# Two token streams on one core: where the second stream stands during attention, and when both streams' scores are emitted

## The chip, the core and the metric

The kernel runs on one core of a Trainium2 chip. The metric is the device time of one execution in microseconds, taken as the median of several executions. The engines are named as in the profile: PE (TensorE matmuls), PEld (TensorE weight loads), DVE (VectorE), ACT (ScalarE), POOL (GpSimd), SP (SyncE, which issues the DMAs).

## What is computed

Four layers of one block (layers 0 to 3) and then two layers of a second block, on 256 tokens of width 1024, in float32. Cut to what matters here:

```python
for i in range(4):                       # first block
    q, k, v, ... = split(x @ w_in[i])    # kind i % 3: indexed top-k, dilated, plain causal
    mix = attention(rope(q), rope(k), v) # 12 heads of 64 columns
    mo  = memory_attention(qm, mk, mv)   # 4 heads over 256 memory tokens
    x = layer_norm(a * x + concat(mix, mo) @ w_out[i])
    x = layer_norm(a * x + swiglu(x, w_gate_up[i], w_down[i]))
for l in range(2):                       # second block: three attentions, gates, output
    u = rms_norm(x) @ w_in_2[l]
    oa, ob, oc = diff_attention, mla_attention, sliding_window_attention
    x = x + rms_norm(gated_sum(oa, ob, oc) @ w_out_2[l]); x = x + gate(x) * (p[l] @ w_ple_proj[l])
```

In layers 0 and 3 each query first scores all keys with 8 small index heads, and keeps the 64 best keys; the attention of the layer sees only those.

## The kernel before

**Two streams.** The 256 tokens are two halves of 128, stream 0 and stream 1, each run by a generator of its own (`stream(t)`, t = 0 or 1). Stream 0 attends to its own 128 keys, stream 1 to all 256, so stream 1's scores are twice as wide. Both use the same weights. These are read from memory in units of 256 rows by 512 columns or less (`Unit`; there are 600). `ensure` issues a unit's DMA on SP into a `raw` buffer (3 of them), has ACT cast it to a high part H (line 333) and DVE subtract that from it to a low part L (line 334); H and L have 7 buffers each. `gemm_part` then makes, for each of a unit's two blocks of 128 rows, three matmuls (H by the high part of x, L by the same, H by the low part, lines 378 to 380): six matmuls for a unit and a stream. The loop at the end of the program takes a unit of stream 0, splits the weights that it needs, and lets stream 1 go on while its unit's place in the sequence is at most that of stream 0 minus `LAG`, which is 4. So each unit is used by stream 0 and, four units later, by stream 1.

**What sets the order of the attention.** After each unit of a stream `tick(t)` moves that stream's clock on by one, and runs what was put off to that time by `defer` and `job`. A head job of two heads a side has the stages a (score matmuls into two PSUM tiles `w`, then the softmax on DVE and ACT, `softmax_of`), b (transposes of the probabilities on PE, line 500, then a copy) and c (matmuls with the values, line 511, then the division by the sums), one unit of its stream apart. `job` starts one job a stream after the other. So in the code a stage of stream 0 stands directly behind a unit of stream 0, and the same stage of stream 1 behind the same unit of stream 1, four units later.

**Scores.** A score matmul (line 476) contracts over 64 rows, half of the array. `scores` emits, for two sides of heads, a matmul on the upper 64 rows and one on the lower 64 in turn. Each of them appears as two rows in the trace, so x4 in the order is x8 in the trace. Each stream has two PSUM tiles `w`, used for scores, for transposes and for the values' result, and two tiles `mm` for the units.

**Index selection.** In layers 0 and 3 `index_jobs` makes the index scores of 8 heads in two groups (ACT's Relu at line 768, sums on DVE at lines 771 and 773), then eight rounds of the eight largest (line 782) and their replacement (line 783) on DVE, two rounds at a unit, and a mask.

**Softmax.** With a mask or bias DVE adds it and finds the minimum (line 487); without one (the memory heads) it finds the minimum alone (line 483). ACT takes the exponential (line 491). Both engines do their work in the order of the program, and the casts and subtractions of weights are between.

Of the kernel before, what the change touches and what calls it, by code (L numbers as in the profile page):

```python
# [31 lines left out]

LAG = 4
QI_WAIT = 2
IDX_WAIT = 1
# [16 lines left out]
class Unit:  # L52
    def __init__(self, chunk, kt0, nkt, seq):
        self.chunk, self.kt0, self.nkt, self.seq = chunk, kt0, nkt, seq

# [10 lines left out]
def tile_two_blocks(  # L66
# [157 lines left out]

    seq = [0]

    def add_units(ck, groups, step=2, at=None):
        made = []
        for g0, gn in groups:
            for k0 in range(g0, g0 + gn, step):  # L230
                made.append(len(units))
                units.append(Unit(ck, k0, min(step, g0 + gn - k0), seq[0] if at is None else at))
                seq[0] += at is None
        return made
# [11 lines left out]
    def out_chunks(w, late):  # L246
        cks = [Chunk(w, [(0, 512)]), Chunk(w, [(512, 1024)])]
        early = [g for g in ((0, 4), (6, 2)) if g[0] != late] if late == 4 else [(0, 2), (6, 2)]
        order = [add_units(ck, early) for ck in cks]
        rest = [(4, 2)] if late == 4 else [(2, 4)]  # L250
        return cks, order, [add_units(ck, rest) for ck in cks]

    plan1, plan2 = [], []
    for i in range(DEPTH):
# [3 lines left out]
        if kind == 0:  # L258
            pl["qi"] = chunk(w, (2304, 2816))
            pl["wk"] = chunk(w, (2816, 3144))  # L260
            pl["v0"] = chunk(w, (1536, 2048))
            pl["v1"] = chunk(w, (2048, 2304))
        else:
            pl["v1"] = chunk(w, (2048, 2560))
            pl["v0"] = chunk(w, (1536, 2048))
        if kind == 1:
# [24 lines left out]
    for l in range(DEPTH_2):  # L291
        pl = {}
        w = w_in_2[l]
        pl["b"] = chunk(w, (2048, 2464))
        pl["aq"] = chunk(w, (0, 512))
# [6 lines left out]
        pl["zb"] = chunk(w, (2464, 2976))  # L302
        pl["za"] = chunk(w, (1536, 2048))
# [42 lines left out]

    def job(t, *stages, span=1):
        at = max(now[t] + 1, started[t] + 1)
        started[t] = at + span - 1
        for k, fn in enumerate(stages):  # L350
            defer(t, fn, at=at + k)
        return at + len(stages)

    def tick(t):
        now[t] += 1
        run_until(t, now[t])

    def run_until(t, at):
        q = queues[t]
        while q and q[0][0] <= at:  # L360
            heapq.heappop(q)[2]()

    def finish(t, at):
        while queues[t] and queues[t][0][0] <= at:
            heapq.heappop(queues[t])[2]()

# [277 lines left out]
    def attend_job(t, nk, *sides):  # L644
# [3 lines left out]
        def a():  # L648
            made = scores(t, *[(d["q"], d["k"]) for d in sides])
            for x, d, s in zip(st, sides, made):  # L650
                x["sums"] = d["sums"] if "sums" in d else small(2, "sums", bufs=4)
                bias = d.get("bias")
                x["sm"] = softmax_of(t, s, n, nk, bias() if callable(bias) else bias, x["sums"],
                                     inits=d.get("inits"), mins=d.get("mins"))

# [6 lines left out]

        return job(t, a, b, *[lambda i=i: c(i) for i in range(len(sides))], span=len(sides))


    def block1(t):
# [6 lines left out]
        for i in range(DEPTH):  # L673
# [42 lines left out]
            def dilated_job(s0):  # L716
# [16 lines left out]
                def a0():  # L733
                    made = scores(t, *sides((0, 1)))
                    for (_, _, d), s in zip(heads, made):
                        d["sm"] = work_tile([P, 3, nk], "sm", 2)
                        d["mn"], d["sum"] = small(3, "mn3"), small(1, "rsum")
                        masked(d, s, 0, 0)
                        masked(d, s, 1, 1)

                def a1():
                    made = scores(t, *sides((2,)))
                    for (_, _, d), s in zip(heads, made):
                        masked(d, s, 0, 2)
                        sm = d["sm"]
                        act.activation(sm, sm, AF.Exp, bias=d["mn"][:, 2:3], scale=-1.0, accum_out=d["sum"])
                        vec.tensor_tensor(out=sm[:, 1], in0=sm[:, 1], in1=sm[:, 2], op=ALU.add)
                        vec.tensor_tensor(out=sm[:, 0], in0=sm[:, 0], in1=sm[:, 1], op=ALU.add)

# [8 lines left out]

                return job(t, a0, a1, b, c, span=2)

            def index_jobs(wi):
                def group(g):
                    halves = [([4 * g + e, 4 * g + 2 + e], half_slice(e)) for e in range(2)]
                    made = scores(t, *[([qiT[r, h // 2, :] for h in hs], [[k[r, :] for k in kiTs]] * 2)
                                       for hs, r in halves])
                    for (hs, _), s in zip(halves, made):
                        rl = work_tile([P, 2, nk], "sm", 2)
                        act.activation(rl, s[:, :, :nk], AF.Relu)
                        for e, h in enumerate(hs):
                            if h == 0:  # L770
                                vec.tensor_scalar(score[:, :nk], rl[:, e], wi[:, 0:1], None, op0=ALU.mult)
                            else:
                                vec.scalar_tensor_tensor(out=score[:, :nk], in0=rl[:, e], scalar=wi[:, h : h + 1],
                                                         in1=score[:, :nk], op0=ALU.mult, op1=ALU.add)

# [74 lines left out]
            if kind == 1:  # L850
                for s in range(2):
                    for c, dst in enumerate((qT, kT)):
                        acc = yield from gemm(t, pl["qk"][2 * s + c], *xT)
# [6 lines left out]
            else:  # L860
                for g in range(3):
                    acc = yield from gemm(t, pl["qk"][g], *xT)
                    nat = q_evac(acc, 512)
# [15 lines left out]
            else:  # L879
                ek, lk = ((0, 4), (6, 2)), (4, 2)  # L880
            run_until(t, max(ends[:-1]))
            end = ends[-1]
# [45 lines left out]
    def block2(t):  # L928
# [4 lines left out]
        for l in range(DEPTH_2):  # L933
# [99 lines left out]
            def diff_job(h0):  # L1033
                st = {}

                def a():
# [4 lines left out]
                                        [[s[2][r, h0 + e, :] for s in sh] for e in range(2)]) for r in rows])  # L1041
                    for m in range(2):
                        st[m] = softmax_of(t, made[m], 2, nk, [bias[:, e, :] for e in range(2)],
                                           st["sums"][:, 2 * m : 2 * m + 2])
                    rc = small(4, "r4")
                    vec.reciprocal(rc, st["sums"])
                    vec.tensor_scalar(rc[:, 2:4], rc[:, 2:4], nlam[:, l : l + 1], None, op0=ALU.mult)
                    for e in range(2):
                        vec.tensor_scalar(st[1][:, e], st[1][:, e], rc[:, 2 + e : 3 + e], None, op0=ALU.mult)
                        vec.scalar_tensor_tensor(out=st[0][:, e], in0=st[0][:, e], scalar=rc[:, e : e + 1],  # L1050
                                                 in1=st[1][:, e], op0=ALU.mult, op1=ALU.add)

# [153 lines left out]
    def pos(i):  # L1206
        if i is None:
            return 2 - LAG
        return units[i].seq if i < END else seq[0]

    want1 = None
    while True:
# [4 lines left out]
        cur[0] = 1  # L1217
        while want1 != END and (i0 == END or pos(want1) <= pos(i0) - LAG):
# [55 lines left out]
```

## Time and profile before

| what | value |
|---|---|
| median of 3 runs | 1944.62 us (1942.68 to 1945.63) |
| profiled execution | 1942.13 us, its span 1940.4 us |
| granted TensorE clock | 0.999 of full speed |
| PE busy | 1899.5 us, 98% of the span |
| PE weight loads | 1575.2 us, 81% |
| DVE, ACT, POOL busy | 1241.3, 968.5, 205.1 us (64%, 50%, 11%) |
| DMA | 169 GB/s over the span |

The slices of the page show PE at nine tenths or more in every slice but the first and the last, and DVE between five and eight tenths. Times in the views are us from the start of the span. A matmul's own duration overlaps the next one's, so the time that one costs is read from start to start.

### The profile page before, as it was taken

The numbers are of one execution on the slowest core, as the hardware profiler recorded it, in microseconds if no ns is written. First come the engines' busy times: TensorE is split into PE (matmuls) and PEld (weight loads), VectorE is DVE, ScalarE is ACT, GpSimd is POOL, SyncE is SP. The second block draws the span as 40 slices with busy tenths as digits, with TensorE's granted clock in tenths as the row PEclk, the third lists the DMA queues.
The fourth block names the chain that finished last, engine by engine and source line by source line (L and its number), as shares of the span: only waits on it lengthen the run. The fifth ranks groups of instructions, "written<-read, shape, count | busy, mean of one in ns | idle before, by whom it ended". The sixth has DMA issues, their size and how long they took to land. (4 is left out here: it accounts for less than half of the span.)

```text
span 1940.4 us, 26934 instructions
## 1 busy us (share of the span) xinstructions
PE 1899.5 (98%) x9821; PEld 1575.2 (81%) x9821; DVE 1241.3 (64%) x2136; ACT 968.5 (50%) x1630; POOL 205.1 (11%) x358
## 2 busy tenths in 40 slices
PE   7999999999999999999999999999999999999998
PEld 6888788888888887888877788887888887888886
DVE  5857565657665565755568575657675667576565
ACT  5654444455444455444445544436664456665453
POOL 4010000011000011000020100002120111111010
PEclk9999999999999999999999999999999999999999
DMA  6635665544665553565554265555455655445653
GB/s 199 185 110 163 212 208 185 187 137 151 206 186 184 194 169 103 185 187 185 192 169 142 98 190 188 182 187 173 116 165 176 193 175 163 120 145 162 186 183 109
DMA packets 198293, 327.52 MB, mean 169 GB/s; under 512 B 12914, under 2 KB 70838, under 8 KB 198160
## 3 DMA queue, kind: packets, MB, share of 16 engines
q1 hardware_dynamic: 191072, 306.03, 49.8%
q0 software_dynamic: 5312, 17.44, 2.9%
q10 hardware_dynamic: 1776, 2.33, 0.4%
q8 instruction: 77, 1.26, 0.3%
q14 instruction: 56, 0.46, 0.1%
HBM read 324.68 MB, written 3.43 MB: 169 GB/s over the span
## 5 line engine op out<-in xcount | busy, mean ns | idle before, releaser
L334 DVE TENSOR_TENSOR L<-raw,H 128x1024 fp32r<-128x1024 f32 (+2 forms) x600 | 726.0, 1210 | 450.3 <-ACT H L333 448.2
L333 ACT CAST H<-raw 128x1024 fp32r<-128x1024 f32 (+2 forms) x600 | 612.9, 1022 | 581.9 <-PE mm L380 493.7
L378 PE MATMUL mm<-H,xH 128*128 128x512 f32 (+3 forms) x1840 | 730.0, 398 | 2.1 <-ACT H L333 1.8
L380 PE MATMUL mm<-H,xL 128*128 128x512 f32 (+4 forms) x1840 | 709.5, 387 | 2.1 <-DVE xL L409 1.7
L379 PE MATMUL mm<-L,xH 128*128 128x512 f32 (+3 forms) x1840 | 707.9, 385 | 0.0
L380 PEld LDWEIGHTS mm<-H,xL 128*128 128x128 f32 x1840 | 346.3, 188 | 72.2 <-DVE xL L409 3.4
L378 PEld LDWEIGHTS mm<-H,xH 128*128 128x128 f32 x1840 | 347.1, 189 | 69.7 <-ACT xH L416 3.3
L379 PEld LDWEIGHTS mm<-L,xH 128*128 128x128 f32 x1840 | 347.7, 189 | 58.1
L378 PE MATMUL mm<-H,hH 128*128 128x512 f32 x352 | 137.8, 391 | 0.0
L379 PE MATMUL mm<-L,hH 128*128 128x512 f32 x352 | 137.2, 390 | 0.0
L380 PE MATMUL mm<-H,hL 128*128 128x512 f32 x352 | 137.1, 390 | 0.0
L426 POOL TENSOR_SCALAR pw_in<-mv 128x1 f32<-128x1 f32 x22 | 13.1, 598 | 817.5 <-DVE mv L435 817.5
L491 ACT ACTIVATE sm<-sm,mn 128x128 f32<-128x128 f32 (+1 forms) x136 | 60.4, 446 | 40.5 <-DVE mn L487 40.2
L401 PE MATMUL w<-cst,nat 128*128 128x128 f32 (+1 forms) x436 | 70.4, 276 | 8.5 <-POOL nat L220 3.9
L380 PEld LDWEIGHTS mm<-H,hL 128*128 128x128 f32 x352 | 66.1, 188 | 13.8
L379 PEld LDWEIGHTS mm<-L,hH 128*128 128x128 f32 x352 | 66.1, 188 | 13.4
L378 PEld LDWEIGHTS mm<-H,hH 128*128 128x128 f32 x352 | 66.1, 188 | 13.3
L401 PEld LDWEIGHTS w<-cst,nat 128*128 128x128 f32 (+1 forms) x436 | 52.3, 138 | 28.9 <-POOL nat L220 9.1
L217 POOL TENSOR_TENSOR rope<-nat,rc 128x128 f32<-128x128 f32 (+1 forms) x38 | 21.6, 569 | 312.9 <-ACT nat L626 263.8
L416 ACT CAST xH<-w 128x512 fp32r<-128x512 f32 (+1 forms) x64 | 33.0, 530 | 42.8 <-PE w L401 41.1
L500 PE MATMUL w<-cst,sm 128*128 128x128 f32 x304 | 48.1, 276 | 2.6 <-ACT sm L491 2.5
L907 ACT ACTIVATE nat<-mm 128x512 f32<-128x512 f32 (+1 forms) x48 | 27.0, 562 | 44.5 <-PE mm L380 44.5
(262 smaller groups left out, 1945.5 us busy)
## 6 DMA issues: line engine op xcount, KB each, us to landing
raw<-in_w_gate_up_dram SPq DMA_DIRECT2D x160, 512.0 KB, 3.7
raw<-in_w_in_dram SPq DMA_DIRECT2D x104, 512.0 KB, 3.5
raw<-in_w_down_dram SPq DMA_DIRECT2D x88, 512.0 KB, 3.5
raw<-in_w_out_dram SPq DMA_DIRECT2D x48, 512.0 KB, 3.5
raw<-in_w_in_a_dram SPq DMA_DIRECT2D x56, 256.0 KB, 2.9
raw<-in_w_in_a_dram SPq DMA_DIRECT2D x16, 512.0 KB, 4.3
raw<-in_w_mem_kv_dram SPq DMA_DIRECT2D x16, 512.0 KB, 4.0
raw<-in_w_gate_up_dram SPq DMA_DIRECT2D x32, 256.0 KB, 2.9
```

The lines of the kernel that those rows point to most:

```text
L217: eng.tensor_tensor(out=t1, in0=v, in1=bc(c), op=ALU.mult)
L333: act.copy(h, raw)
L334: vec.tensor_tensor(out=lo, in0=raw, in1=h.bitcast(F32), op=ALU.subtract)
L378: pe.matmul(a, xh[:, kt, :], h[:, j, :], start=st, stop=False)
L379: pe.matmul(a, xh[:, kt, :], lo[:, j, :], start=False, stop=False)
L380: pe.matmul(a, xl[:, kt, :], h[:, j, :], start=False, stop=en)
L401: pe.transpose(tr[:width, j, :], src(j), ident)
L416: act.copy(h, tr[:, :n, :])
L426: pool.tensor_scalar(v[:, :n], src, eps, None, op0=ALU.add)
L491: act.activation(sm[:, j, :], src, AF.Exp, bias=mn[:, j : j + 1], scale=-1.0, accum_out=sums[:, j : j + 1])
L500: pe.transpose(tr[:, j * nkt + kt, :], sm[:, j, kt * P : (kt + 1) * P], ident)
L907: act.activation(a, acc[:, :n], AF.Tanh, scale=0.5)
```

## The change

From a layer's first chunk behind the index queries (or the second part of the values, or the first narrow chunk of the second block) to the layer's output matmuls, units carry the lag `NEAR = 1`; elsewhere 4. The score stages of jobs with more than one side are no longer run at their time but put on a list, `held`. The main loop releases the list after each step of both streams, and so does `run_until` before another stage of the same stream with a later due time. At a release all the score matmuls on the list are emitted first, the last one put on the list first (stream 1's), then all the softmaxes (`rest`) in the same order. In `scores` the two sides change places. Line numbers of the kernel after: 417 to 419 are the units' matmuls, 515 the scores, 539 the transposes of probabilities, 345 the subtraction L.

```diff
+NEAR = 1
...
+            lag[0] = NEAR
             pl["wk"] = chunk(w, (2816, 3144))
...
+        lag[0] = LAG
         pl["za"] = chunk(w, (1536, 2048))
...
         for k, fn in enumerate(stages):
-            defer(t, fn, at=at + k)
+            if k < score:
+                defer_scores(t, fn, at=at + k)
+            else:
+                defer(t, fn, at=at + k)
         return at + len(stages)
...
+    held = []
+
+    def defer_scores(t, fn, after=1, at=None):
+        at = now[t] + after if at is None else at
+        defer(t, lambda: held.append((t, at, fn)), at=at)
+
+    def release(t=None, at=None):
+        if not held or t is not None and all(h[0] != t or h[1] >= at for h in held):
+            return
+        todo, was = list(held), cur[0]
+        held.clear()
+        rest = []
+        for t, _, fn in reversed(todo):
+            cur[0] = t
+            rest.append((t, fn()))
+        for t, fn in rest:
+            cur[0] = t
+            fn()
+        cur[0] = was
...
-    def run_until(t, at):
-        q = queues[t]
+    def run_until(t, at, made=None):
+        q, later = queues[t], []
         while q and q[0][0] <= at:
-            heapq.heappop(q)[2]()
...
+            item = heapq.heappop(q)
+            if made is not None and item[1] > made:
+                later.append(item)
+                continue
+            release(t, item[0])
+            item[2]()
...
-                for s, (qs, kss) in zip(made, sides):
+                for s, (qs, kss) in reversed(list(zip(made, sides))):
...
         def a():
             made = scores(t, *[(d["q"], d["k"]) for d in sides])
-            for x, d, s in zip(st, sides, made):
...
+            def rest():
+                for x, d, s in zip(st, sides, made):
...
+            return rest
...
                 for g in range(2):
-                    defer(t, lambda g=g: group(g), after=IDX_WAIT + 1 + g)
+                    defer_scores(t, lambda g=g: group(g), after=IDX_WAIT + 1 + g)
...
     def pos(i):
-        if i is None:
-            return 2 - LAG
         return units[i].seq if i < END else seq[0]
...
+        return pos(i) <= pos(i0) - units[i].lag
...
+        release()
```

The first place is PE's order at the second group of heads of layer 3. `xH_8740` is stream 0's x, `xH_8837` stream 1's; the score matmuls in pairs of rows are stream 1's (`x2` rows, two key blocks), the row `x4` stream 0's. Before:

```order
L380 MATMUL mm<-H,xL_8838 128x512
L476 MATMUL w<-b_0_8760,b_1_8857 128x128 x2
L476 MATMUL w<-b_1_8857 128x128 x2
L476 MATMUL w<-b_0_8760,b_1_8857 128x128 x2
L476 MATMUL w<-b_1_8857 128x128 x2
L378 MATMUL mm<-H,xH_8740 128x512
L379 MATMUL mm<-L,xH_8740 128x512
L380 MATMUL mm<-H,xL_8741 128x512
L378 MATMUL mm<-H,xH_8740 128x512
L379 MATMUL mm<-L,xH_8740 128x512
L380 MATMUL mm<-H,xL_8741 128x512
L476 MATMUL w<-b_0_8760 128x128 x4
```

and after:

```order
L419 MATMUL mm<-H,xL_8838 128x512
L515 MATMUL w<-b_0_8760,b_1_8857 128x128 x2
L515 MATMUL w<-b_1_8857 128x128 x2
L515 MATMUL w<-b_0_8760,b_1_8857 128x128 x2
L515 MATMUL w<-b_1_8857 128x128 x2
L515 MATMUL w<-b_0_8760 128x128 x4
L417 MATMUL mm<-H,xH_8740 128x512
```

Stream 0's four score matmuls have moved up to stream 1's eight, past a unit of stream 0; two rows of scores between units are one.

The second place is the transposes of the same heads' probabilities, on PE a few rows on. Before:

```order
L380 MATMUL mm<-H,xL_8838 128x512
L500 MATMUL w<-cst,sm 128x128 x8
L378 MATMUL mm<-H,xH_8740 128x512
L379 MATMUL mm<-L,xH_8740 128x512
L380 MATMUL mm<-H,xL_8741 128x512
L378 MATMUL mm<-H,xH_8740 128x512
L379 MATMUL mm<-L,xH_8740 128x512
L380 MATMUL mm<-H,xL_8741 128x512
L500 MATMUL w<-cst,sm 128x128 x4
```

and after:

```order
L418 MATMUL mm<-L,xH_8837 128x512
L419 MATMUL mm<-H,xL_8838 128x512
L417 MATMUL mm<-H,xH_8837 128x512
L418 MATMUL mm<-L,xH_8837 128x512
L419 MATMUL mm<-H,xL_8838 128x512
L539 MATMUL w<-cst,sm 128x128 x12
L417 MATMUL mm<-H,xH_8740 128x512
```

Stream 0's four transposes have moved up to stream 1's eight, past a unit of stream 0; between the scores and all twelve transposes stand two units' matmuls (12).

The third place is DVE in layer 3, where the index selection ends. `b2_0_8761` is stream 0's index score, `b2_1_8858` stream 1's; `L_...` rows are weight units, `mn_...` the first minima of the memory heads. Before:

```order
L334 TENSOR_TENSOR L_9323<-raw_9319,H_9322 128x1024
L773 SCALAR_TENSOR_TENSOR b2_1_8858<-sm_9225,wi_9092,b2_1_8858 128x256 x2
L773 SCALAR_TENSOR_TENSOR b2_1_8858<-sm_9229,wi_9092,b2_1_8858 128x256 x2
L779 TENSOR_TENSOR b2_1_8858<-b2_1_8858,cst_83 128x256
L782 MAX m8_9260<-b2_1_8858 128x8
L783 MATCH_REPLACE b2_1_8858<-m8_9260,b2_1_8858 128x256
L334 TENSOR_TENSOR L_9362<-raw_9358,H_9361 128x1024
L782 MAX m8_9263<-b2_1_8858 128x8
L334 TENSOR_TENSOR L_9397<-raw_9393,H_9396 128x1024
L783 MATCH_REPLACE b2_1_8858<-m8_9263,b2_1_8858 128x256
L483 TENSOR_REDUCE mn_9309<-w_9301 128x2
L782 MAX m8_9289<-b2_1_8858 128x8
```

and after, the end of the selection:

```order
L839 MAX m8_9278<-b2_0_8761 128x8
L839 MAX m8_9301<-b2_1_8858 128x8
L840 MATCH_REPLACE b2_0_8761<-m8_9278,b2_0_8761 128x128
L840 MATCH_REPLACE b2_1_8858<-m8_9301,b2_1_8858 128x256
L839 MAX m8_9281<-b2_0_8761 128x8
L843 TENSOR_SCALAR b2_1_8858<-b2_1_8858 128x256
L840 MATCH_REPLACE b2_0_8761<-m8_9281,b2_0_8761 128x128
L844 TENSOR_TENSOR b2_1_8858<-b2_1_8858,cst_83 128x256
L843 TENSOR_SCALAR b2_0_8761<-b2_0_8761 128x128
L345 TENSOR_TENSOR L_9408<-raw_9404,H_9407 128x1024
L844 TENSOR_TENSOR b2_0_8761<-b2_0_8761,cst_83 128x128
L522 TENSOR_REDUCE mn_9362<-w_9348 128x2
```

After, the eight rounds of both streams stand in turn between two weight units, with no unit among them, and the minima of the memory heads stand behind all of them; before, weight units and minima stand between stream 1's rounds.

## Rows read from the trace of the kernel before

**Rows 1.** Page, part 1: busy time, share of the span, instructions of each engine

```profile
PE 1899.5 (98%) x9821; PEld 1575.2 (81%) x9821; DVE 1241.3 (64%) x2136; ACT 968.5 (50%) x1630; POOL 205.1 (11%) x358
```

**Rows 2.** Waits of PE: what waited for what, us in total, times, longest

```profile
PE w L401 <- POOL nat L220: 3.9, 8, 1.1
PE w L819 <- DVE ki L813: 3.4, 3, 2.1
...
PE w L500 <- ACT sm L491: 2.5, 3, 1.9
```

**Rows 3.** Timeline of PE, layer 3's second heads: start, us, engine, line, operation

```profile
1072.63 0.40 PE L380 MATMUL mm<-H,xL 128*128 128x512 f32 x1
1072.96 0.49 PE L476 MATMUL w<-b,b 64*128 64x128 f32 x4
...
1074.39 0.40 PE L379 MATMUL mm<-L,xH 128*128 128x512 f32 x1
...
1075.32 0.39 PE L380 MATMUL mm<-H,xL 128*128 128x512 f32 x1
1075.63 0.71 PE L476 MATMUL w<-b 64*128 64x128 f32 x8
1076.28 0.50 PE L378 MATMUL mm<-H,xH 128*128 128x512 f32 x1
1076.62 0.39 PE L379 MATMUL mm<-L,xH 128*128 128x512 f32 x1
...
1077.78 1.04 PE L500 MATMUL w<-cst,sm 128*128 128x128 f32 x8
1078.57 0.47 PE L378 MATMUL mm<-H,xH 128*128 128x512 f32 x1
```

**Rows 4.** Timeline of ACT, the same place

```profile
1073.11 1.05 ACT L333 CAST H<-raw 128x1024 fp32r<-128x1024 f32 x1 [1.06 <-PE mm L380]
1075.85 0.51 ACT L491 ACTIVATE sm<-sm,mn 128x256 f32<-128x256 f32 x1 [1.70 <-DVE mn L487]
...
1077.84 0.39 ACT L491 ACTIVATE sm<-sm,mn 128x128 f32<-128x128 f32 x1
...
1078.99 0.39 ACT L491 ACTIVATE sm<-sm,mn 128x128 f32<-128x128 f32 x1
```

**Rows 5.** Timeline of DVE, the same place

```profile
1074.19 1.23 DVE L334 TENSOR_TENSOR L<-raw,H 128x1024 fp32r<-128x1024 f32 x1 [1.68 <-ACT H L333]
1075.33 0.42 DVE L487 CUSTOM_DVE_ANT_0 sm<-w,b 128x256 f32<-128x256 f32 x1
```

**Rows 6.** Timeline of PE, layer 0: eight score rows of one stream that do not pair

```profile
129.99 0.48 PE L476 MATMUL w<-b,b 64*128 64x128 f32 x2
...
131.08 0.51 PE L379 MATMUL mm<-L,xH 128*128 128x512 f32 x1
```

**Rows 7.** Timeline of PE, layer 3's memory heads: scores, then the transposes' wait

```profile
1037.03 1.14 PE L476 MATMUL w<-mkv,b 64*128 64x256 f32 x8
...
1042.41 0.33 PE L500 MATMUL w<-cst,sm 128*128 128x128 f32 x1 [1.95 <-ACT sm L491]
```

**Rows 8.** Timeline of DVE, layer 3: rounds of the selection, both widths, and a minimum

```profile
1028.34 0.29 DVE L782 MAX8 m<-b 128x8 f32<-128x128 f32 x1
...
1028.94 1.22 DVE L334 TENSOR_TENSOR L<-raw,H 128x1024 fp32r<-128x1024 f32 x1
...
1040.62 0.68 DVE L483 TENSOR_REDUCE mn<-w 128x2 f32<-128x512 f32 x1
...
1042.65 0.43 DVE L782 MAX8 m<-b 128x8 f32<-128x256 f32 x1
...
1043.52 1.22 DVE L334 TENSOR_TENSOR L<-raw,H 128x1024 fp32r<-128x1024 f32 x1
```

**Rows 9.** Groups of DVE by line and form: count, busy us, mean ns

```profile
L773 DVE SCALAR_TENSOR_TENSOR b<-sm,wi,b 128x256 f32<-128x256 f32 x14 | 6.7, 476 | 0.2
...
L773 DVE SCALAR_TENSOR_TENSOR b<-sm,wi,b 128x128 f32<-128x128 f32 x14 | 4.9, 350 | 1.0 <-ACT sm L768 0.7
```

More of the change, by code (lines that the diff above doesn't have):

```diff
@@ L225, in tile_two_blocks @@
     seq = [0]
+    lag = [LAG]
     def add_units(ck, groups, step=2, at=None):
@@ L231, in add_units @@
                 made.append(len(units))
-                units.append(Unit(ck, k0, min(step, g0 + gn - k0), seq[0] if at is None else at))
+                units.append(Unit(ck, k0, min(step, g0 + gn - k0), seq[0] if at is None else at, lag[0]))
                 seq[0] += at is None
@@ L248, in out_chunks @@
         early = [g for g in ((0, 4), (6, 2)) if g[0] != late] if late == 4 else [(0, 2), (6, 2)]
-        order = [add_units(ck, early) for ck in cks]
+        order = []
+        for ck in cks:
+            order.append(add_units(ck, early))
+            if late == 4:
+                lag[0] = LAG
+        lag[0] = LAG
         rest = [(4, 2)] if late == 4 else [(2, 4)]
@@ L345, in defer, with job @@
         heapq.heappush(queues[t], (now[t] + after if at is None else at, count[0], fn))
-    def job(t, *stages, span=1):
+    def job(t, *stages, span=1, score=1):
         at = max(now[t] + 1, started[t] + 1)
@@ L356, in tick @@
         run_until(t, now[t])
-    def run_until(t, at):
-        q = queues[t]
+    def run_until(t, at, made=None):
+        q, later = queues[t], []
         while q and q[0][0] <= at:
-            heapq.heappop(q)[2]()
-    def finish(t, at):
-        while queues[t] and queues[t][0][0] <= at:
-            heapq.heappop(queues[t])[2]()
+            item = heapq.heappop(q)
[4 more added lines that the diff above has]
+            item[2]()
+        for item in later:
+            heapq.heappush(q, item)
     def gemm_part(t, acc, ids, xh, xl, first, last):
@@ L661, in c @@
             sides[i]["done"](pv(st[i]["pt"], n, nk, sides[i]["v"]), st[i]["sums"])
-        return job(t, a, b, *[lambda i=i: c(i) for i in range(len(sides))], span=len(sides))
+        pair = len(sides) > 1
+        return job(t, a if pair else lambda: a()(), b, *[lambda i=i: c(i) for i in range(len(sides))],
+                   span=len(sides), score=int(pair))
     def block1(t):
@@ L765, in group, with rest @@
                                        for hs, r in halves])
[L766 to L774, printed above, removed]
+                    def rest():
+                        for (hs, _), s in zip(halves, made):
+                            rl = work_tile([P, 2, nk], "sm", 2)
+                            act.activation(rl, s[:, :, :nk], AF.Relu)
+                            for e, h in enumerate(hs):
+                                if h == 0:
+                                    vec.tensor_scalar(score[:, :nk], rl[:, e], wi[:, 0:1], None, op0=ALU.mult)
+                                else:
+                                    vec.scalar_tensor_tensor(out=score[:, :nk], in0=rl[:, e], scalar=wi[:, h : h + 1],
+                                                             in1=score[:, :nk], op0=ALU.mult, op1=ALU.add)
+                    return rest
                 def select(r0, r1):
@@ L880, in block1 @@
                 ek, lk = ((0, 4), (6, 2)), (4, 2)
-            run_until(t, max(ends[:-1]))
+            run_until(t, max(ends[:-1]), made)
             end = ends[-1]
@@ L1041, in a, with rest @@
                                         [[s[2][r, h0 + e, :] for s in sh] for e in range(2)]) for r in rows])
[L1042 to L1051, printed above, removed]
+                    def rest():
+                        for m in range(2):
+                            st[m] = softmax_of(t, made[m], 2, nk, [bias[:, e, :] for e in range(2)],
+                                               st["sums"][:, 2 * m : 2 * m + 2])
+                        rc = small(4, "r4")
+                        vec.reciprocal(rc, st["sums"])
+                        vec.tensor_scalar(rc[:, 2:4], rc[:, 2:4], nlam[:, l : l + 1], None, op0=ALU.mult)
+                        for e in range(2):
+                            vec.tensor_scalar(st[1][:, e], st[1][:, e], rc[:, 2 + e : 3 + e], None, op0=ALU.mult)
+                            vec.scalar_tensor_tensor(out=st[0][:, e], in0=st[0][:, e], scalar=rc[:, e : e + 1],
+                                                     in1=st[1][:, e], op0=ALU.mult, op1=ALU.add)
+                    return rest
                 def b():
@@ L1217, in tile_two_blocks @@
         cur[0] = 1
-        while want1 != END and (i0 == END or pos(want1) <= pos(i0) - LAG):
+        while want1 != END and follows(want1, i0):
             want1 = next(s1, END)
```

48 lines of the change are left out of this document (30 added, 18 removed).

## The prediction

> **What bounds the kernel now.** I read the page's busy times first. PE is busy 98% of the span, DVE 64%, ACT 50% [rows 1], so on the whole the time is PE's row of matmuls, and there are two ways to a shorter one: fewer or cheaper things in the row, or fewer gaps. The list of what PE waited for shows how little is in the gaps of the stages that the change touches: 3.9 us for the rotation on POOL, 3.4 us for the index keys, 2.5 us for the exponentials, in 14 waits together [rows 2]. So the gain has to come from PE's own row, and a gap made in exchange costs its full length.
>
> Next I read PE's timeline start to start, for the price of a row of score matmuls between units. In an undisturbed stretch a unit's matmul takes (1075.32 - 1074.39) / 4 = 0.233 us [rows 3]. From the last matmul of a unit over 16 score rows to the second matmul of the next unit it is 1074.39 - 1072.63 = 1.76 us; without the scores it would be two steps, 0.47, so the scores cost 1.29. Over 8 score rows it is 1.30 - 0.47 = 0.83 us [rows 3]. Eight rows more cost 0.46 us, so 0.83 - 0.46 = **0.37 us is paid once for each row of scores between units**, however short it is. Eight transposes in a row, on the full array, take 0.79 us, 0.1 each, and show no such entry price [rows 3]. This is the cost that the change goes for.
>
> Then the other engines at the same place, for what is late if PE comes sooner. The scores start at 1072.96. A unit's buffer has just come free, so ACT casts first (1073.11, 1.05 us) [rows 4] and DVE subtracts (1074.19, 1.23 us), and only then come the masks, from 1075.33 [rows 5]: 2.37 us after the scores began. The exponentials run from 1075.85 without a pause: stream 1's four 0.5 us each, stream 0's four from 1077.84, the last from 1078.99 for 0.39 us [rows 4], so the probabilities are whole at 1079.38, 6.4 us behind the start. In the order before nothing waits: stream 0's transposes stand a unit of 1.4 us behind stream 1's, which end at 1078.57 [rows 3], so at about 1080.0.
>
> **What the change takes away.** Counting PE's orders of before and after, the rows of scores between other work fall from 89 to 52. 37 x 0.38 (with 0.37 and 0.41 as the ends of what such rows give) = **-14.1 us**, from -13.7 to -15.2.
>
> Pairing: eight score rows on the same half of the array take 1.09 us up to the next unit [rows 6], eight that alternate between the halves 1076.28 - 1075.63 = 0.65 [rows 3]. So a score matmul alone and a pair of opposite ones take one step alike, (1.09 - 0.65) / 2 = 0.22 us (0.43 for 256 columns, as twice the width). By the orders there are 15 fewer steps of 128 columns and one of 256 fewer: 15 x 0.22 + 0.43 = **-3.8 us**. The ends are 0 (pairs that were already overlapped by the neighbour row) and -4.
>
> Rotation waits: behind a unit of the one stream the transposes of queries and keys now regularly have six matmuls of the other ahead of them. Of the 3.9 us [rows 2] I take **-1.5**; the ends are 0 and -3.9. The 3.4 us for the index keys I leave as they are: the chain of small DVE operations ahead of them is the same, the distance about the same.
>
> **What it adds: late softmaxes.** In the joined place the second group's order is 24 score rows, two units (12 matmuls), twelve transposes. PE comes to the transposes at 1.09 + 0.46 (scores) + 12 x 0.233 + 0.1 = 4.45 us behind the start and would be through them at 5.65. ACT and DVE have the same work in the same order as before (cast, subtraction, stream 1's heads, stream 0's), since none of it depends on where stream 0's scores stand, and the last exponential ends at 6.4, the last transpose at 6.5 to 6.7. PE waits 0.9 to 1.1 us. What is queued behind is all of PE: the next unit's matmuls stand behind the transposes. There are eight such places, two in layer 0 and three each in layers 2 and 3: 8 x 1.0 = **+8.0 us**. The ends are 0 (if the cast and subtraction come earlier, the masks could start at 1.1 instead of 2.37, and the chain ends at 5.2) and 8 x 1.5 (one more DVE operation in between).
>
> The memory heads are four sides of 256 columns with minima of 0.68 us [rows 8] on DVE; before, one stream's two sides came at a time. In layers 1 and 2 I take 1.0 each, like the heads. In layer 3 the wait was already 1.95 us [rows 7], 2.8 with what followed it; I take 3.7. Together **+2.9**, from 0 to +8. The sliding windows of the second block have two places of the same form: **+2.0**, from 0 to +2.4. The dilated heads of layer 1 have two score stages behind each other and come out even (0.3 at most).
>
> The index selection: a round takes DVE (1043.52 - 1042.65) = 0.87 us for stream 1 and 1028.94 - 1028.34 = 0.60 for stream 0 [rows 8]. Eight of each are 11.8 us, with the last sums, 4 x 0.476 + 4 x 0.350 [rows 9], 15 us. Before, five or six weight units and the memory heads' minima were between them; after, they stand as one block between two units. Seven buffers of two streams' work at 2 x 1.4 us each are 19.6 us, so in layer 3, with full units, the block fits and it is the memory heads' minima that come late (counted above). In layer 0 the units at this place are narrow and the buffers are just filling: the next weight unit comes 4.9 us late where before 2.8 were lost: **+2.0**, from 0 to +7.
>
> In the second block scores now stand directly behind transposes and value matmuls that use the same two PSUM tiles of their stream, and wait until these are copied away: **+1.3**, from 0 to 2.6. DMAs are the same in number, size and order; SP's issues go with the buffers as before.
>
> The sum: -14.1 - 3.8 - 1.5 + 8.0 + 2.9 + 2.0 + 2.0 + 1.3 = -3.2. On the profiled execution's 1942.1 that is 1938.9; the median of the runs is 2.5 us above it, so **1941.4 us**, 0.16% less than before. It is a change of -19 us paid back by +16.
>
> Weighed against a rule: at the joined place eight heads' exponentials hold ACT for 3.5 us (1075.85 to 1079.38) [rows 4], while PE needs 1.55 us for the scores. The Trainium skill, page TensorEngine Tiling (Array Packing), section PSUM Bottleneck, says that small tiles speed up TensorE but not the emptying of PSUM, which may become the limit. By it alone a joined row would gain nothing anywhere, and the time would be the old one, 1944.6; by the rows PE's entry price goes in any case and comes back only where the transposes stand too near.
>
> **The rivals.**
>
> *The softmaxes keep up.* If the scheduler's buffers come free earlier at the joined places, so that cast and subtraction don't stand ahead of the masks, the chain ends at 5.2 us, before PE would be through its transposes at 5.65, and the heads' and windows' 10 us are not paid. Against it: the cast waits on PE's last use of the buffer [rows 4], which is the unit ahead of the scores in both orders. Time: -3.2 - 10 = -13.2, **1931.4 us**.
>
> *Slower: the index selection holds the weights and the memory heads.* In layers 0 and 3 DVE gets both streams' rounds in one block. If stream 1's eight rounds (7.0 us) all fall on PE, through the minima or the next units' L, instead of the 2.9 that I have there (2.0 and 0.9), the sum is -3.2 - 2.9 + 14 = +7.9: **1952.5 us**. It decides as soon as the block ends more than 3 us later than the buffers' 19.6 us allow, in both layers. For it: the wait in layer 3 stands in the trace already with one stream's rounds in the way [rows 7, 8]. Against it: DVE is idle a third of the time [rows 1].
>
> *The way back to the wide lag.* At the end of each layer's attention stream 0 goes ahead alone for three units. A unit alone takes PE 1.4 us, while DVE's subtraction takes 1.23 [rows 5] and has the softmaxes and norms beside it. If each of the six layers loses 1 us there: +2.8, **1947.4 us**. It would be called no change.
>
> *That the change doesn't do what it says* is excluded by the order: the rows of scores are joined.
>
> **How the numbers follow.** Some 0.2%, 3.9 us, is what a measurement can tell from no change: faster is below 1940.7, slower above 1948.5. My forecast, late softmaxes that eat most of the gain, 0.48, 1937 to 1946; the softmaxes keep up 0.24, 1924 to 1937; the selection 0.18, 1949 to 1956; the way back 0.10, 1945 to 1950. Faster: 0.24 and something over four tenths of my own case, 0.44. Slower: 0.18, and 0.07 of the others, 0.25. Same: 0.31. The range leaves out the lower third of the softmaxes' case and the upper part of the selection's: 1929 to 1951.
>
> **What would show it.** Right: PE's busy time some 15 us or more below 1899.5; waits of the probabilities' transposes for the exponentials, 2.5 us now [rows 2], grow to 10 or more, in eight to fourteen waits of about 1 us. If they stay at 2.5, the first rival; if the minima or L rows of layers 0 and 3 are what PE waits for, with 5 us or more in one place, the second. If PE's busy time does not fall, the entry price of a score row was not what the pairs of rows say, and the sum fails at its first term.

## The result

The changed kernel takes 1955.63 us (median of 4 runs, 1951.04 to 1956.74) against 1944.99 us of the kernel before beside it: a ratio of 1.0051, with a 95% interval from 1.0037 to 1.0066. It is slower by half a per cent, 10.6 us by the medians, where 0.16% faster was forecast, and the time lies above the range of 1929 to 1951 us.

The page of the profiled execution after (1955.76 us, its span 1954.0 us), part 1, with the columns of [rows 1]:

```profile
PE 1891.2 (97%) x9821; PEld 1575.2 (81%) x9821; DVE 1236.4 (63%) x2130; ACT 970.6 (50%) x1636; POOL 208.3 (11%) x358
```

PE is busy 8.3 us less than in [rows 1], and the span is 13.6 us longer: PE's idle time went from 40.9 to 62.8 us. What it waited for after (us in total, times, longest), to be held against [rows 2]:

```profile
PE w L539 <- ACT sm L530: 18.3, 15, 3.0
PE w L440 <- POOL nat L221: 10.4, 10, 2.1
```

Probabilities' transposes (line 539) wait 18.3 us for exponentials, where it was 2.5, and transposes of rotated rows (line 440) 10.4 us for POOL, where it was 3.9. These two are 22.3 us more, as much as the whole growth of the idle time.

The place of [rows 3 to 5] in the kernel after, PE's timeline:

```profile
1093.75 0.39 PE L419 MATMUL mm<-H,xL 128*128 128x512 f32 x1
1094.07 0.49 PE L515 MATMUL w<-b,b 64*128 64x128 f32 x4
...
1095.61 0.50 PE L417 MATMUL mm<-H,xH 128*128 128x512 f32 x1
...
1099.48 1.70 PE L539 MATMUL w<-cst,sm 128*128 128x128 f32 x12 [0.85 <-ACT sm L530]
```

and ACT's at the same place:

```profile
1094.22 1.04 ACT L344 CAST H<-raw 128x1024 fp32r<-128x1024 f32 x1 [2.40 <-PE mm L419]
1096.96 0.51 ACT L530 ACTIVATE sm<-sm,mn 128x256 f32<-128x256 f32 x1 [1.70 <-DVE mn L526]
...
1100.10 0.39 ACT L530 ACTIVATE sm<-sm,mn 128x128 f32<-128x128 f32 x1
```

The scores start at 1094.07, two units follow, and PE could begin the transposes at about 1098.5, but the last exponential ends at 1100.49, 6.4 us after the scores began. This is the place as the prediction drew it, to the tenth.

A thing that it did not draw is what PE's clock does behind a long wait, here at the memory heads of layer 2. The first group is PE's timeline; the second is the busy time of each engine in stretches of 2 us, whose third column from the right is the granted clock:

```profile
717.93 0.66 PE L539 MATMUL w<-cst,sm 128*128 128x128 f32 x4 [2.95 <-ACT sm L530]
...
721.27 0.63 PE L418 MATMUL mm<-L,xH 128*128 128x512 f32 x1
721.70 0.63 PE L419 MATMUL mm<-H,xL 128*128 128x512 f32 x1
```

```profile
717.00:719.00 2.00, 1.07 (x7) 0.82 (x8) 0.50 (x3) 2.00 (x9) 0.00 (x0) 1.00 0.26 89
719.00:721.00 2.00, 2.00 (x12) 2.00 (x12) 1.41 (x2) 1.81 (x3) 0.00 (x0) 0.58 0.01 4
721.00:723.00 2.00, 2.00 (x7) 1.57 (x6) 1.06 (x2) 0.00 (x0) 0.00 (x0) 0.57 0.18 35
723.00:725.00 2.00, 2.00 (x15) 1.78 (x14) 0.29 (x1) 0.00 (x0) 0.00 (x0) 1.00 0.67 227
```

PE waited 2.95 us, and then ran at half clock (1.2 instead of 2.4 GHz) for (0.42 + 0.43) x 2 / 0.5 = 3.4 us, which costs half of that, 1.7 us: a unit's matmul takes 721.70 - 721.27 = 0.43 us there, not 0.23. There are four such stretches between the first and the last unit in the profile after (at 88, 238, 719 and 1057 us), one in that of before (at 21 us): 3 x 1.7 = 5.1 us more.

### The profile page after: what moved, and what is told of

Its sections match the earlier page's. It is cut to its first block, busy times and chain, and to the rows that moved or that the text cites. A ratio compares the mean times of both kernels' runs of the same rounds, so it can differ in the third digit from the quotient of the medians.

```text
span 1954.0 us, 26917 instructions
## 1 busy us (share of the span) xinstructions
PE 1891.2 (97%) x9821; PEld 1575.2 (81%) x9821; DVE 1236.4 (63%) x2130; ACT 970.6 (50%) x1636; POOL 208.3 (11%) x358
## 5 line engine op out<-in xcount | busy, mean ns | idle before, releaser
L440 PE MATMUL w<-cst,nat 128*128 128x128 f32 (+1 forms) x436 | 69.9, 277 | 15.0 <-POOL nat L221 10.4
L419 PEld LDWEIGHTS mm<-H,hL 128*128 128x128 f32 x352 | 66.1, 188 | 13.6
L417 PEld LDWEIGHTS mm<-H,hH 128*128 128x128 f32 x352 | 66.1, 188 | 13.5
L418 PEld LDWEIGHTS mm<-L,hH 128*128 128x128 f32 x352 | 66.1, 188 | 13.5
L539 PE MATMUL w<-cst,sm 128*128 128x128 f32 x304 | 51.2, 290 | 19.4 <-ACT sm L530 18.3
L539 PEld LDWEIGHTS w<-cst,sm 128*128 128x128 f32 x304 | 36.0, 148 | 32.3 <-ACT sm L530 26.4
```

The lines of the kernel that those rows point to most:

```text
L417: pe.matmul(a, xh[:, kt, :], h[:, j, :], start=st, stop=False)
L418: pe.matmul(a, xh[:, kt, :], lo[:, j, :], start=False, stop=False)
L419: pe.matmul(a, xl[:, kt, :], h[:, j, :], start=False, stop=en)
L440: pe.transpose(tr[:width, j, :], src(j), ident)
L539: pe.transpose(tr[:, j * nkt + kt, :], sm[:, j, kt * P : (kt + 1) * P], ident)
```

## The experiments

All runs are compared with the kernel before on the same chip; its medians there were 1944.0, 1944.3, 1944.1 and 1944.6 us. Three parts of the change can be told apart: the sides of a score row change places; `run_until` at a layer's end no longer runs stages that were put off after the last chunk's start (`made`); and the narrow lag with the held scores.

**The change taken apart.** `sides_only` is the changed kernel with lag 4 and nothing held, so that the first two parts are left:

```diff
-NEAR = 1
+NEAR = 4
...
-        defer(t, lambda: held.append((t, at, fn)), at=at)
+        defer(t, lambda: fn()(), at=at)
```

> Lag 4 everywhere and nothing held: what is left of the change is that the two sides of a score row change places, and small changes in when the stages at a layer's end run. Theory: as the kernel before, less up to eight score rows (81 where that has 89) at 0.38 us: 1940 to 1945 us. Rival (the changed places of the sides cost a part of the loss): 1948 us or more.

It measured 1933.58 us, a ratio of 0.9945 (0.9928 to 0.9961): 10.4 us faster than before, more than either side expected. So the change holds a gain that needs neither the lag nor the holding, and the rest of it costs 22 us, not 11. Which of the two parts gains? `before_sides` is the kernel before with the sides exchanged:

```diff
-                for s, (qs, kss) in zip(made, sides):
+                for s, (qs, kss) in reversed(list(zip(made, sides))):
```

> The kernel before with one line changed: the two sides of a score row change places (stream and lag as before, nothing held). Theory (the changed places give what the run with lag 4 and nothing held gained, 10 us): 1933 to 1938 us. Rival (the gain is from the third part, the stages at a layer's end that are no longer run early, since by the order this kernel has 90 score rows and that one 81): 1941 to 1946 us.

1940.70 us, 0.9982 (0.9973 to 0.9991). The theory falls; the sides give 3.6 us. `kept_only` is the kernel before with the second part:

```diff
-            run_until(t, max(ends[:-1]))
+            run_until(t, max(ends[:-1]), made)
```

> The kernel before with only the third part: at a layer's end, stages that were put off after the last chunk's start are no longer run early (81 score rows by the order, 89 before). Sides, lag and scores as before. If this part gives what the run with lag 4 and nothing held has beyond the changed places of the sides (1933.6 against 1940.7): 1936 to 1939 us. Rival (it gains only together with the changed places): 1942 to 1945 us.

1936.82 us, 0.9963 (0.9949 to 0.9976): 7.3 us, as expected. 3.6 and 7.3 add to 10.9, within the scatter of the 10.4 that both bring together. Now the lag alone, with nothing held (only the second half of the diff of `sides_only`):

> The scores are no longer held: each stream emits its own where they come due; the lag stays 1. By PE's order the heads' scores are joined all the same (54 score rows where the changed kernel has 52), only the memory heads' come apart. Theory (late exponentials and the clock they cost): the memory heads' waits, about 11 us in four layers, fall to 5 or less, three of the four stretches at half clock go (1.7 us each), the eight head waits of 1 us stay: 1945 to 1949 us. Rival (the narrow lag with its crowding of the small engines is the cause, the memory heads' waits only move): 1953 to 1957 us.

The count in this expectation is wrong: the trace has 84 score rows, the heads' scores are not joined, so the run is the narrow lag without the joining. It measured 1952.01 us (1.0036, 1.0023 to 1.0049), between the two ranges, and that is **18.4 us more than with lag 4**. The same waits in both, first lag 4, then lag 1:

```profile
PE w L440 <- POOL nat L221: 2.3, 6, 0.9
...
PE w L539 <- ACT sm L530: 1.9, 3, 1.4
```

```profile
PE w L440 <- POOL nat L221: 10.1, 9, 2.1
...
PE w L539 <- ACT sm L530: 4.0, 6, 1.3
```

The rotation's waits are there before anything is joined; of the exponentials' 18.3 us only 4.0 are. Lag 3 with nothing held:

> The changed kernel with a lag of 3 in attention and nothing held. Theory (the narrower the lag, the more the small work of both streams meets on POOL, ACT and DVE): between lag 4 (1933.6) and lag 1 (1952.0), 1936 to 1942 us, waits for the rotation between 2.3 and 10.1 us. Rival (only lag 1, where both streams' stages stand in the same unit, costs): 1931 to 1935 us.

1945.62 us (1.0006, 0.9996 to 1.0016), slower than both ranges. Waits for the rotation were 6.5 us. Lag 3 costs 12 of lag 1's 18 us: it is not only lag 1 that costs, and the cost does not grow in proportion to the units taken off the lag. Held scores at lag 4:

```diff
-NEAR = 1
+NEAR = 4
```

> Lag 4 everywhere, scores held and joined where stages of both streams come due in one step (76 score rows by the order, 81 without holding). Theory (the narrow lag is the larger part of the loss, holding gives back in late transposes about what its rows save): 1932 to 1938 us. Rival (holding is the larger part at any lag): 1942 us or more.

1938.66 us (0.9973, 0.9962 to 0.9985), a little above the theory's range and well under the rival's: holding costs 5.1 us at lag 4, where it joins 81 rows into 76 only, and 1955.6 - 1952.0 = 3.6 us at lag 1, where it joins 84 into 52. (The runs of the two kernels at lag 1 overlap, 1951.0 to 1956.7 and 1949.6 to 1952.8 us, so the 3.6 is rough.) The lag is the larger part.

**Holding.** `mem_apart` leaves the memory heads' scores unheld:

```diff
-        pair = len(sides) > 1
+        pair = len(sides) > 1 and "bias" in sides[0]
```

> The changed kernel, but the memory heads' scores are not held; the other heads' are. Theory: the memory heads' waits of 2 to 3 us in all four layers (11 us) fall to 4 or less, and the three stretches at half clock behind them (1.7 us each) go; two more score rows: 1942 to 1947 us. Rival (the wait moves to what comes next, the other heads): 1952 us or more.

1948.79 us (1.0023, 1.0014 to 1.0032), 6.8 us less than the changed kernel, just past the theory's range. The exponentials' wait is 11.7 us in 17 times, none over 1.6 us, and one stretch at half clock is left, at 21 us as in the profile before. So joining the other heads gains 1952.0 - 1948.8 = 3.2 us, and joining the memory heads loses 6.8. `late_T` puts the later stages of all held jobs off by one unit:

```diff
-                defer(t, fn, at=at + k)
-        return at + len(stages)
+                defer(t, fn, at=at + k + int(score > 0))
+        return at + len(stages) + int(score > 0)
```

> The transposes of the probabilities and the value matmuls of held jobs come one unit later; scores stay held. Theory: the 18.3 us of waits for exponentials fall below 4, three stretches at half clock go (1.7 us each), nine more score rows cost 3.4: 1938 to 1944 us. Rival (the wait only moves, to scores that wait for PSUM tiles still in use by transposes or value matmuls): 1950 us or more, with the wait on score rows.

1957.01 us (1.0067, 1.0052 to 1.0082): the rival's number, but not its place. The transposes' waits for exponentials fell from 18.3 to 4.3 us, about as the theory had it, and others grew:

```profile
PE w L440 <- POOL nat L221: 13.0, 9, 3.1
PE w L539 <- ACT sm L530: 4.3, 5, 1.9
...
PE w L550 <- ACT sm L530: 2.3, 1, 2.3
```

with six stretches at half clock and nine more score rows.

**The rotation.** `rope_late` gives the rotated queries of the second block one unit more:

```diff
-                defer(t, lambda qn=qn, e=e: head_T(qn, mqT[:96, 4 * e : 4 * e + 4, :], MLA_QSCALE))
+                defer(t, lambda qn=qn, e=e: head_T(qn, mqT[:96, 4 * e : 4 * e + 4, :], MLA_QSCALE), 2)
```

> In the second block the transposes of the rotated queries come one unit later than in the changed kernel; nothing else is changed. Theory: of the 10.4 us of waits for POOL's rotation the 7.5 in the second block fall below 2: 1948 to 1952 us. Rival (POOL's rotation is slowed by DVE's weight subtraction, and the next stage takes over the wait): 1954 to 1957 us.

1956.00 us (1.0055, 1.0037 to 1.0073), nothing gained: POOL's waits fell to 6.9 us, but 2.2 us appeared for POOL's next copy of keys, and the profile has six stretches at half clock, one of them of double length, where the changed kernel's has four. `rope_dve` moves this rotation from POOL to DVE:

```diff
-                rope(t, qn[:, :, 64:96], 1)
+                rope(t, qn[:, :, 64:96], 1, vec)
```

> The changed kernel, but the rotation of the second block's 96-wide queries runs on DVE in place of POOL (four operations of each of eight rotations). Theory (with both streams a unit apart POOL's rotations, lengthened beside DVE's weight subtraction, are late; 6.5 us of the 10.4 us of waits for POOL are there): 1948 to 1952 us, waits for POOL's rotation under 5 us. Rival (DVE in the same place is as late, since it has both streams' work too): 1954 us or more.

1948.54 us (1.0022, 1.0012 to 1.0032), 7.1 us less; POOL's waits are 2.8 us, the exponentials' 18.6 as before. Why POOL is late is in the changed kernel's rows in the second block, POOL first, then DVE, then PE:

```profile
1368.36 1.36 POOL L218 TENSOR_TENSOR rope<-nat,rc 128x128 f32<-128x128 f32 x1 [18.02 <-ACT nat L1066]
1369.68 0.31 POOL L219 TENSOR_TENSOR rope<-nat,rs 128x64 f32<-128x64 f32 x1
...
1370.35 1.50 POOL L221 TENSOR_TENSOR nat<-rope,rope 128x128 f32<-128x128 f32 x1
1371.81 0.45 POOL L218 TENSOR_TENSOR rope<-nat,rc 128x128 f32<-128x128 f32 x1
```

```profile
1368.18 1.22 DVE L345 TENSOR_TENSOR L<-raw,H 128x1024 fp32r<-128x1024 f32 x1
1370.31 1.22 DVE L345 TENSOR_TENSOR L<-raw,H 128x1024 fp32r<-128x1024 f32 x1 [0.92 <-ACT H L344]
```

```profile
1371.90 0.64 PE L440 MATMUL w<-cst,nat 128*96 128x128 f32 x4 [2.10 <-POOL nat L221]
```

The two POOL operations that lie beside a weight subtraction take 1.36 and 1.50 us, the same first operation clear of one 0.45. At 0.45 each the rotation would have been through 2.0 us sooner (an estimate from these rows), nearly the whole wait of 2.10 us. In the whole profile after, 24 of the 41 operations of this size at lines 218 and 221 that overlap a weight subtraction take over 0.5 us, up to 1.5, and none of the 19 that don't takes over 0.47. The Trainium skill, page GPSIMD Engine Reference, section Specifications, says that GpSimd shares its interfaces to SBUF, the on-chip memory, with VectorE, and that there is contention with VectorE instructions that have two inputs there. The subtraction has two, raw and H, and the trace agrees. The slowing itself is not new: before, one rotation of this place has an operation of 1.34 us, and PE waits 0.21 us for it. New is how close the rotations stand: before, the four start at 1354.68, 1357.19, 1365.24 and 1368.54 us, after at 1368.36, 1371.81, 1373.56 and 1375.06, with no pause of POOL between. The same edit with lag 1 and nothing held:

> Lag 1, nothing held, and the second block's query rotation on DVE. Theory (the rotation is the largest single part of the narrow lag's cost): 7 us less than the 1952.0 with POOL, 1943 to 1947 us, so some 10 us of the lag's cost are elsewhere. Rival (the rotation's 7 us came only with the joined scores): 1949 us or more.

1944.89 us (1.0002, 0.9993 to 1.0011), 7.1 us less than with POOL, as the theory had it.

**Both at once, and later.** `apart_rope` joins the edits of `mem_apart` and `rope_dve`:

> The changed kernel with two causes taken away at once: the memory heads' scores not held, and the second block's query rotation on DVE. Theory (the two add): 1948.8 less what the rotation alone brings, 4 to 7 us: 1942 to 1945 us, the eight head waits of 1 us still there. Rival (what one takes away the other brings back): 1947 us or more.

1938.71 us (0.9978, 0.9967 to 0.9989): 16.9 us less than the changed kernel, where 6.8 and 7.1 add to 13.9; the 3 us between are within the scatter of the runs. Its profile has no stretch at half clock between the first and the last unit. The waits are

```profile
PE w L539 <- ACT sm L530: 11.4, 16, 1.5
...
PE w L440 <- POOL nat L221: 3.6, 4, 1.4
```

On top of it, `heads_later` and `all_later` put the later stages of the heads in layers 0, 2 and 3, and of the sliding windows too, off by a unit (`late_T`'s edit for these jobs):

> As the run with memory heads apart and rotation on DVE (1938.7), and the transposes and value matmuls of the heads in layers 0, 2 and 3 one unit later. Theory (the eight waits of 1 us come from the transposes standing two units behind the scores): waits for exponentials fall from 11.4 to 4 us or less, two more score rows: 1931 to 1935 us. Rival (as when all held jobs came later: the wait moves to rotation, PSUM tiles or the layer's end): 1937 us or more.

> As heads_later, and the same for the sliding windows of the second block (two waits of 1 us): 1.5 to 2 us less than that run, 1929 to 1934 us. Rival (the end of the attention then waits for the later values): the same as that run or more.

1938.08 us (0.9969, 0.9955 to 0.9982) and 1939.42 us (0.9977, 0.9966 to 0.9987). The exponentials' waits fell to 3.8 and 2.1 us, and the time stayed. Read from start to start between `apart_rope` and `heads_later`, PE has 9.0 us less ahead of the probabilities' transposes, and 3.2 us more ahead of other transposes, 2.9 us more on score rows and 3.0 us more ahead of value matmuls. The rival holds: the wait moves. Why it moves there was not tried.

**The fastest.** `best` is `sides_only` with the rotation on DVE:

> Lag 4, nothing held, sides changed, stages kept back at a layer's end, and the second block's query rotation on DVE: a candidate for the fastest. POOL's waits are only 2.3 us there without it, so 0 to 2 us less than 1933.6: 1931 to 1934 us. Rival (four more DVE operations delay the weights' subtraction): 1935 us or more.

1931.45 us (median of 5; 0.9935, 0.9922 to 0.9947): 12.7 us faster than before and 24 faster than the changed kernel, with lag 4 and nothing held. What the rotation on DVE adds at lag 4, 2.1 us, is hardly clear of the scatter: `sides_only` ran from 1931.7 to 1934.7 us, this from 1929.2 to 1932.6.

## Why the prediction was wrong, point by point

The runs put the time together so (medians): 1944.3 before; sides -3.6; stages kept back -7.3 (together 1933.6); lag 1 +18.4 (1952.0); holding the heads -3.2 (1948.8); holding the memory heads +6.8 (1955.6). By the intervals of the runs each step is good to some 2 to 4 us. The forecast of 1941.4 failed first of all by what it left out, the cost of the narrow lag itself.

*The entry price of a score row, right.* From the last matmul ahead of a row to the second behind it, less the undisturbed steps of such matmuls, the 89 rows before cost 92.4 us, and the 52 after 73.5 (with 1.7 and 0.4 us of waits in them): -18.9, where -14.1 - 3.8 = -17.9 was forecast. The same reading gives 87.2 us in `kept_only` (81 rows), 86.2 in `sides_only` (81), 87.2 in `near_only` (84) and 73.7 in `mem_apart` (54). So 6.2 us of it came without any joining. Joining the heads took 13.5 us off PE's row, of which the time kept 3.2: the waits for exponentials grew from 4.0 to 11.7. PE's busy time fell by 8.3 us, not by the 15 that was to show it right; most of the difference is the clock, since at 1.7 us for each of three more stretches it would have fallen by 13.4.

*The late heads and windows, right.* Measured from start to start over the undisturbed gap, seven of the eight head places lose 0.91 to 1.01 us, 6.9 together, for +8.0 (one of layer 0's two shows no wait); the two windows 1.01 each, for +2.0. The chain of cast, subtraction, masks and exponentials ahead of the transposes is as it was drawn. That the way out, one unit later, gives nothing (`heads_later`), was not foreseen.

*The rotation, wrong in sign.* The prediction took -1.5 us, since a unit of the other stream now stands ahead of each transpose. It looked at PE's order, and not at POOL, which gets the next rotation directly behind the last and is slowed beside DVE's subtraction. Measured: +6.5 us of waits, and 7.1 us of time by `rope_dve`.

*The narrow lag was never costed as itself; the step that failed most.* The prediction read it as what joins the rows, and put its costs at the joined places. `near_only` shows 18.4 us with nothing joined. With the rotation on DVE in both, lag 1 is still 1944.9 - 1931.5 = 13.4 us slower than lag 4. By the profiles' layers (from the last addition of the layer before to the last addition behind the attention) 3.9 us of it are in layer 0, 4.5 in layers 2 and 3, 4.0 in the second block. Between the two profiles PE's waits are 6.8 us more (5.1 of them for exponentials and rotation, 1.5 for L in layer 0, the others go both ways), and PE's busy time is 6.8 us more (1898.1 against 1891.3): 1.7 for one stretch at half clock, 2.3 on score rows, of which there are three more. The last 2.8 us stay open.

*The first heads of layer 0* had no term. They are not joined, and PE waits there for the exponentials of stream 0, ACT first, then PE:

```profile
85.13 1.28 ACT L530 ACT_TABLE_LOAD   x1
```

```profile
86.97 0.33 PE L539 MATMUL w<-cst,sm 128*128 128x128 f32 x1 [2.01 <-ACT sm L530]
```

ACT loads a table, 1.28 us, before its first exponential. The load is in every profile, but PE waits at this place, 1.27 to 2.21 us, only in those with lag 1 whose transposes are not put off by a unit; in `before`, `sides_only`, `best` and `lag3` it does not. So this is a part of the narrow lag's cost in layer 0, not of the joining.

*The memory heads, mis-sized.* +2.9 was forecast, 1 us for each of two layers, 0.9 in layer 3, nothing in layer 0, where they are not joined. The waits after are 2.29 and 2.95 us in layers 1 and 2, and 0.96 with 1.89 in layer 3, each for exponentials; before there were 0.25 in layer 1 and 1.95 with 0.26 in layer 3. That is 5.6 us more, and `mem_apart` gains 6.8 us. At the wait of 2.95 us DVE and ACT do this, DVE first:

```profile
713.17 1.22 DVE L345 TENSOR_TENSOR L<-raw,H 128x1024 fp32r<-128x1024 f32 x1 [1.50 <-ACT H L344]
714.31 2.47 DVE L522 TENSOR_REDUCE mn<-w 128x2 f32<-128x512 f32 x4
```

```profile
712.09 1.05 ACT L344 CAST H<-raw 128x1024 fp32r<-128x1024 f32 x1 [1.68 <-DMA raw<-in_w_in_c_dram]
715.03 0.47 ACT L530 ACTIVATE sm<-w,mn 128x256 f32<-128x256 f32 x1 [1.89 <-DVE mn L522]
...
718.19 0.51 ACT L530 ACTIVATE sm<-w,mn 128x256 f32<-128x256 f32 x1
```

A cast, which waits for its unit's DMA, and the subtraction stand ahead of the minima, and then ACT has eight exponentials, 0.45 us apart, stream 1's four first. Taking the place for one like the heads missed that. The two engines' orders are also opposed: PE's first transposes start at 717.93, right behind the sixth exponential, stream 0's second, though stream 1's four were whole at 716.96. With stream 1's transposes first PE could start up to 0.9 us sooner here (an estimate from these rows; not tried). Two of these three places, in layers 2 and 3, are followed by half clock.

*The clock, left out.* None of the terms had it. Three more stretches are 5.1 us of the profile's 13.6; the mean granted clock of the four runs after was 0.994 to 0.998, that of all runs of the kernel before 0.996 to 1.0.

*The stages kept back and the sides.* `before_sides` gains 3.6 us, close to the pairing's -3.8, but its score rows cost only 0.7 us less than before (91.7 us for 90 rows); that its gain is the pairing's is not shown. The second part was in the diff that the prediction quotes, and had no term of its own: it gains 7.3 us. Its eight rows fewer are 5.1 of that by the reading above, and stood unnoticed in the count of 37.

*The small terms.* The index selection's +2.0 came about as drawn: in layer 0 DVE makes the rounds of both streams with no subtraction of a weight unit from 57.1 to 68.0 us, and behind them PE waits 1.53 us for L. It does so with nothing held too (1.37 us in `near_only`), so this also belongs to the lag. The second block's +1.3 for PSUM tiles did not come: no score row waits there. The waits for the index keys, left as they were, fell from 3.9 to 1.9 us, by luck as far as the forecast goes.

*The rivals.* The softmaxes don't keep up: 18.3 us of waits where 2.5 were. The index selection (1952.5) comes near the time for another reason: its wait for L is 1.53 us and not 5, layer 3, where it should decide, is 0.2 us shorter than before up to the end of its attention (144.3 against 144.6 us), and layer 0 is 2.2 longer. The way back to the wide lag (1947.4) names the lag, but not the place: in the profile after PE waits for a weight unit's H or L only at 19 and at 69 us, and at no layer's end. That a joined row gains nothing, which would give the old time, is too little for the heads, which gain 3.2 us, and too much for the memory heads, which lose 6.8.

## What to carry to other kernels

Joining work on the busiest engine saves its entry price, and whatever it makes late gives it back; the price was right to about 1 us here, and the sum was wrong by what the small engines did. When a change brings two streams of work closer in time, cost the closeness itself: list for each small engine (POOL first) what of both streams now stands in one unit, and which operations of another engine lie beside it. Take a diff apart by its lines, and cost the lines that look like bookkeeping: here the part worth keeping, 7.3 us, had no term of its own, and with the exchanged sides, lag 4 and the rotation on DVE it makes a kernel that is 0.65% faster than before.

## What the runs showed of the hardware

The stretch at half clock is 3.4 us long each time between the first and the last unit of these profiles (6.8 us once in `rope_late` and once in `all_later`), and 3.4 us of it cost 1.7. In the profile after it followed waits of PE of 2.01, 2.24 and 2.95 us, and a pair of 0.96 and 1.89 us with 0.44 us of work between; it did not follow waits of 2.29 us (layer 1) and 2.10 us (second block, twice). One of the four, at 238 us, is in the feed-forward part that the change doesn't touch: a wait of 2.24 us for DVE, where before it was 1.70 and no such stretch followed. In `near_only` the same wait of 2.10 us in the second block, at 1364.74, was followed by one, and in `rope_dve` a wait of 3.51 us at the memory heads of layer 2 was not. So the length of one wait doesn't settle it.

It also makes much of the scatter between executions of one kernel. The ten of `rope_dve` go from 1941.98 us at a mean clock of 0.999 over 1948.5 at 0.997 to 1951.2 at 0.994. 0.005 of the clock is 0.005 x 1945 = 9.7 us, and 9.2 were measured. Not all scatter is of this kind: of the ten of `mem_apart` one at 0.995 took 1948.69 us and one at 0.999 1948.44.
